# Two convolution blocks made in halves among the last attention heads, with a different opening, in an encoder layer on one core

## The chip, the core and the metric

The kernel runs on one core of a Trainium2 chip, as one program and one launch. Its engines are TensorE (matrix products; PE in the profile, with PEld for the loading of weights), VectorE (DVE), ScalarE (ACT), GpSimd (POOL) and SyncE (SP), which here only issues DMA transfers. Each engine works through its own list of instructions in order, and they wait for each other by semaphores. A transfer waits in the queue of the engine that issues it until its buffer is free, and whatever is behind it in that queue waits too. The metric is device time in microseconds.

## What is computed

One layer of a streaming encoder, in f32, over a sequence of 1024 positions and 1024 features:

```python
mod = (c_act @ w_ada[l] + b_ada[l])[:, None, :]
sh_m, sc_m, g_m, sh_f, sc_f, g_f = jnp.split(mod, 6, axis=-1)
h = rmsnorm(x, norm_mix_w[l]) * (1 + sc_m) + sh_m
z, xbc, dt_raw, q, k, v = jnp.split(h @ w_in[l], IN_SPLITS, axis=-1)
y_ssd = ssd_mixer(z, xbc, dt_raw, ...)
y_att = chunk_attention(q, k, v, rel_bias[l])
x = x + g_m * (jnp.concatenate([y_ssd, y_att], axis=-1) @ w_out[l])
h = rmsnorm(x, norm_ffn_w[l]) * (1 + sc_f) + sh_f
x = x + g_f * conv_ffn(h, w_up[l], ffn_conv_w[l], w_down[l])
return rmsnorm(x, final_norm_w)
```

Two parts matter here. The attention has 8 heads of 64, and a chunk of 64 positions sees itself and the 8 chunks before it, with a relative bias. The SSD mixer begins with a causal convolution over 4 positions and a silu:

```python
xbc = jax.nn.silu(causal_dwconv(xbc, conv_w) + conv_b.astype(xbc.dtype))
```

Its 1024 channels are eight blocks of 128: 0 to 3 are the values, 4 and 5 the two groups of B, 6 and 7 those of C.

## The kernel before

**Products.** A product of two f32 matrices is made as three faster ones: both operands are split into a rounded high part and the rest, and high by high, high by low and low by high are summed in PSUM (`mm3`, lines 79 to 81; the splitting is `split`, lines 88 and 89). A weight tile of 128 output columns over the whole contraction (8 blocks `kt` of 128) is loaded, split and paired in `wu_pair`. The product of such a tile with the 1024 positions is 2 halves of 24 products of 512 columns (`gemm_ft`).

**Order.** The order of instructions on each engine is made by the framework when the kernel is built: a planner simulates the program's times and takes what is ready, the earlier line of the program first. Two things bind it. `tc.issue_after(i)` puts an instruction behind `i` on the same engine, and the wrappers V, A and T (VectorE, ScalarE, TensorE) keep the program's order while their `on` is set.

**Opening.** The modulation is made column by column: `mod_col` loads 128 rows of `w_ada` (512 KB) and one VectorE instruction with an accumulator multiplies them by the activated condition and sums. The rows of x come in eight tiles of 128 (`x_load`, 512 KB each), each is squared (`x_square`), turned into 1/rms (`x_rstd`: an addition of EPS on VectorE, a power on POOL) and scaled (`x_scale`). For each contraction block `kt` the loop at line 409 makes two modulation columns (scale SC_M and shift SH_M), loads a block of the first weights (`w_first`, 384 KB), splits it into `wsh` and `wsl`, turns the block of x on TensorE and applies scale and shift (`h_block`: high part on ScalarE, the f32 value on ScalarE, low part on VectorE). With it go q and k of pairs 0 and 1 (`first_qk`) and v of both (`first_v`). The positions are done in two halves `hh`; the first is made while weights arrive, with the last two blocks after the others. Block 0 of the first half is made in two parts of two row tiles: only x tiles 0 and 1 are loaded ahead of the modulation, tiles 2 and 3 after it. TensorE makes 8 and 12 products of the identity (`warm_up`) before that.

**Attention.** The heads are four pairs. For pair p and each of four steps u, `attn_scores` makes scores for two tiles of 128 positions (`scores`), adds the bias (with the row minimum, line 529), takes the exponential (532), its reciprocal sum (534) and scales on POOL (535). `attn_pv` then turns the probabilities on TensorE (561, 564), splits them and multiplies by v (572, 573); line 578 adds the halves into `ya`. The two bias tiles of a pair are loaded on SP's queue at its beginning and their corners masked by POOL (591, 592). For tiles 0 to 2 of pair 0 a part of the bias is loaded early (`bias_early`). q, k and v of pair 2 are written inside pair 1, those of pair 3 inside pair 2 (`GP`: q and k in step 0, v in step 2), and the planner uses them to fill TensorE. A k or q tile needs parts moved between partitions, by transfers on SP's queue (line 230). Pairs 1 and 2 make one modulation column in each step (through the single buffer `rowb`, after the last reciprocal sum). Pair 3 has no products besides its own; its first two steps load and split the weights of convolution blocks 4 and 6.

**Convolution blocks.** After pair 3, `conv_silu` makes a block: two halves of products into one PSUM tile of two banks, ScalarE's first tap over 1024 positions, three VectorE steps for the other taps (line 636), and silu. The order is 4, 6, 5, 7, then 0 to 3, which are turned back to rows. After each, `conv_mods` makes 2 to 4 modulation columns (CMODS, 24 in all) through three buffers `wos`.

**Memory.** q and k tiles come from one pool of 12 (`qkp`, 4 KB a partition each), used first by x; B, C and the values have pools that are made when the attention's have been closed.

## Time and profile before

| | us |
|---|---|
| median of 3 runs | 1205.41 |
| lowest and highest | 1205.05, 1207.55 |
| profiled execution | 1205.95 |
| its span, first to last instruction | 1204.2 |

The stages on the span: opening and first projections 0 to 98, pair 0 from 98, pairs 1 and 2 to some 235, pair 3 and the convolution blocks to 362, then the z projection, the SSD scan with the output projection from 420, and the feed-forward part from about 540 to the end.

A row of a timeline has the start, the time, the engine, the line, the operation, output and inputs with shapes and count, and in brackets how long the engine had stood idle before and for whom. L61 is the line of the wrappers V, A and T. TensorE's ends are modelled: successive products overlap, so the rate shows in their starts. A busy time counts a product for its whole length. "PEclk" is the granted share of TensorE's clock.

### The profile page before, as it was taken

The page shows a single profiled execution, that of the slowest core. Times are in us where ns is not written, and L with a number is a line of the kernel's source. Part 1 is how long each engine was busy: PE and PEld are TensorE (multiplying, and loading weights), DVE is VectorE, ACT ScalarE, POOL GpSimd, SP SyncE. Part 2 cuts the span into 40 slices and gives each one's busy share as a digit, 9 for nine tenths or more (in the row PEclk, how much of TensorE's full clock was granted, in tenths as well). Part 3 has the DMA queues.
Part 4 walks back from the last instruction along what each step waited for, and adds up shares of the span by engine and source line. Part 5 has one row for each costly group of instructions (what it writes and reads, how often), then busy time and mean ns, then how long its engine had stood idle before and what let it go on. Part 6 is the DMA issues. An engine that isn't in the chain of part 4 may idle for free.

```text
span 1204.2 us, 15722 instructions
## 1 busy us (share of the span) xinstructions
PE 1168.7 (97%) x5823; PEld 980.8 (81%) x5823; DVE 909.1 (75%) x1364; ACT 587.5 (49%) x968; POOL 156.5 (13%) x177
## 2 busy tenths in 40 slices
PE   8998999899999899999999999999999999999996
PEld 6777888788889888888788888888888888888885
DVE  7645565775596888658999988898889879766986
ACT  6534564674243757577534443344333445433454
POOL 1002342530000344200000000000000000000522
PEclk8998999999999989999999999999999999999998
DMA  9635434301486322140232323322233378733443
GB/s 357 244 84 136 110 108 116 108 1 36 153 273 222 124 66 93 53 164 30 79 139 98 102 92 105 131 81 98 94 121 114 110 250 299 258 114 122 158 132 149
DMA packets 61293, 160.24 MB, mean 133 GB/s; under 512 B 6608, under 2 KB 7072, under 8 KB 59808
## 3 DMA queue, kind: packets, MB, share of 16 engines
q1 hardware_dynamic: 54160, 134.85, 34.2%
q10 hardware_dynamic: 7056, 24.38, 5.1%
q8 instruction: 46, 0.75, 0.3%
q14 instruction: 31, 0.25, 0.1%
HBM read 121.15 MB, written 28.61 MB: 124 GB/s over the span
## 4 chain that ended last, share of the span: by engine, by line
PE 85%; DVE 8%; issue 3%; DMA 2%; ACT 1%; SPq 1%; POOL 0%; POOLq 0%; DVEq 0%; ACTq 0%
PE wops L827 6%; PE dn L81 5%; PE dn L79 5%; PE dn L80 5%; PE uY L79 5%; PE uY L81 5%; PE uY L80 5%; PE uX L81 3%; PE uX L79 3%; PE uZ L80 3%; PE uZ L79 3%; PE uX L80 3%; PE uZ L81 3%; PE s L79 3%; PE s L80 3%
## 5 line engine op out<-in xcount | busy, mean ns | idle before, releaser
L80 PE MATMUL dn<-w 128*128 128x512 f32 x296 | 108.1, 392 | 0.0
L79 PE MATMUL dn<-w 128*128 128x512 f32 x296 | 108.1, 391 | 0.0
L81 PE MATMUL dn<-w 128*128 128x512 f32 x296 | 100.2, 391 | 0.2 <-DVE w L89 0.2
L79 PE MATMUL uY<-tH,w 128*128 128x512 f32 x248 | 97.2, 392 | 0.0
L80 PE MATMUL uY<-tL,w 128*128 128x512 f32 x248 | 97.0, 391 | 0.0
L81 PE MATMUL uY<-tH,w 128*128 128x512 f32 x248 | 96.9, 391 | 0.0
L1549 POOL TENSOR_TENSOR ya<-ya,xs 128x512 f32<-128x512 f32 x4 | 17.2, 4330 | 557.6 <-ACT xs L1545 557.6
L88 ACT ACTIVATE w<-ya 128x1024 fp32r<-128x1024 f32 (+1 forms) x41 | 39.2, 957 | 87.3 <-PE uY L81 84.2
L827 PE MATMUL wops<-hH,yhl 128*128 128x512 f32 x224 | 73.4, 401 | 0.0
L81 PEld LDWEIGHTS dn<-w 128*128 128x128 f32 x296 | 55.4, 188 | 13.2 <-DVE w L89 1.1
L79 PEld LDWEIGHTS dn<-w 128*128 128x128 f32 x296 | 55.5, 188 | 12.3
L80 PEld LDWEIGHTS dn<-w 128*128 128x128 f32 x296 | 55.5, 188 | 12.2
L535 POOL TENSOR_SCALAR p<-p,st 128x640 f32<-128x640 f32 (+4 forms) x64 | 49.3, 776 | 108.3 <-DVE st L534 95.2
L529 DVE CUSTOM_DVE_ANT_0 p<-s,bias 128x640 f32<-128x640 f32 (+4 forms) x58 | 38.3, 676 | 29.2 <-PE tp L561 10.3
L88 ACT ACTIVATE w<-xs 128x1024 fp32r<-128x1024 f32 (+1 forms) x41 | 39.1, 954 | 37.3 <-PE uY L81 33.3
L89 DVE TENSOR_TENSOR pt<-tp,pt 128x512 fp32r<-128x512 f32 (+2 forms) x72 | 42.0, 596 | 18.1 <-ACT pt L88 17.7
L81 PEld LDWEIGHTS uY<-tH,w 128*128 128x128 f32 x248 | 46.6, 188 | 10.5
L79 PEld LDWEIGHTS uY<-tH,w 128*128 128x128 f32 x248 | 46.5, 188 | 10.3
L80 PEld LDWEIGHTS uY<-tL,w 128*128 128x128 f32 x248 | 46.6, 188 | 10.2
L79 PE MATMUL s<-hH,wh 128*128 128x512 f32 x128 | 50.6, 395 | 1.2 <-DVE ct L636 1.0
L88 ACT ACTIVATE pt<-tp 128x512 fp32r<-128x512 f32 (+2 forms) x72 | 36.8, 525 | 29.9 <-PE tp L561 15.4
L1223 DVE SCALAR_TENSOR_TENSOR a<-cv,pkt,a 128x1023 f32<-128x1023 f32 (+1 forms) x40 | 51.0, 1277 | 0.1
(492 smaller groups left out, 3422.4 us busy)
## 6 DMA issues: line engine op xcount, KB each, us to landing
wos<-in_w_ada_dram SPq DMA_DIRECT2D x24, 512.0 KB, 4.6
gz<-a ACTq DMA_DIRECT2D x10, 1024.0 KB, 5.0
ya<-in_w_up_dram SPq DMA_DIRECT2D x11, 768.0 KB, 4.1
xs<-in_w_up_dram SPq DMA_DIRECT2D x11, 768.0 KB, 4.3
adat<-in_w_ada_dram SPq DMA_DIRECT2D x16, 512.0 KB, 7.6
raws<-in_w_ft_dram SPq DMA_DIRECT2D x14, 512.0 KB, 3.8
qk<-qk SPq DMA_DIRECT2D x56, 128.0 KB, 2.3
gy<-a ACTq DMA_DIRECT2D x10, 512.0 KB, 2.6
```

The source lines that it names most:

```text
L79: T.matmul(ps, lh, rh, start=start, stop=False, skip_group_check=more)
L80: T.matmul(ps, lh, rl, start=False, stop=False, skip_group_check=more)
L81: T.matmul(ps, ll, rh, start=False, stop=stop, skip_group_check=more)
L88: i = A.activation(hi, src, AF.Copy) if ehi is A else ehi.tensor_copy(hi, src)
L89: return i, elo.tensor_tensor(lo, src, f32(hi), ALU.subtract)
L529: V.tensor_tensor_reduce(out=dst, in0=src, in1=bsl, scale=-1.0, scalar=3e38, op0=ALU.add, op1=ALU.min, accum_out=nm)
L535: G.tensor_scalar(pv_, pv_, rr, 1.0, op0=ALU.mult, op1=ALU.mult)
L827: i = op(*a, **k)
L1223: V.scalar_tensor_tensor(a[:, j:S], c[:, 0:S - j], w[2 - j], a[:, j:S], op0=ALU.mult, op1=ALU.add)
L1549: G.tensor_tensor(src, src, fnr[:, halves[1]], ALU.mult)
```

## The change

It moves work and reorders it; the products of the layer stay the same.

- **Memory**: the 12 tiles come from three pools of 4: one tile of four (`qkx`, x tiles 4 to 7, then k of pairs 1 and 3, later `xs`), four (`qkb`, q and high k of pairs 0 and 2, later B and C), four (`qkt`, x tiles 0 to 3, then the rest).
- **Convolution**: blocks 4 and 6 are made in halves by `conv_half`, one in each step of pair 3, through the one accumulator `acc`. The last three columns of the first half are kept (`edge`) for the second half's taps. Their weights are prepared in the last step of pair 2 and the second of pair 3. Their silu comes after blocks 5 and 7.
- **Modulation columns**: pairs 1 and 2 make 16 instead of 8 (2 in each step; 3, 3, 2, 0), the convolution stage 16 instead of 24.
- **Pair 0**: its bias tiles are issued on ScalarE's queue; all masks are pinned behind normalizations on POOL. In the q product of pair 2, contraction blocks 1, 3 and 5 are pinned behind scores 1, 2 and 3 of pair 0.
- **Opening**: four x tiles ahead of the modulation, block 0 made whole, tiles squared on ScalarE, VectorE, ScalarE, VectorE; EPS is added on ScalarE, or inside VectorE's reduction; 26 products of the identity instead of 12; the modulation columns and the low part of the weights of each block are pinned behind a shift, and block 0's high part goes to VectorE.

```diff
-CMODS = (2, 3, 3, 3, 3, 3, 4, 3)
+AMODS = {1: (2, 2, 2, 2), 2: (3, 3, 2, 0)}
+CMODS = (3, 3, 3, 3, 2, 2)
+GPIN = {1: (0, 1), 3: (0, 2), 5: (0, 3)}
-WARM = (8, 12)
+WARM = (8, 26)
...
     def new_pair(p):
-        qk[p] = {n: [qk_tile(F32R) for _ in range(2)] for n in ("q", "kh", "kl")}
+        if p % 2:
+            k4 = qk_four(F32R)
+            t = [qk_tile(qkt, n) for n in (2, 3)] + [k4[:, n, :] for n in range(4)]
+        else:
+            t = [qk_tile(qkb, n) for n in range(4)] + [qk_tile(qkt, n) for n in (0, 1)]
+        qk[p] = {n: t[2 * i:2 * i + 2] for i, n in enumerate(("q", "kh", "kl"))}
...
         if eng is A:
-            i = norm_to(xts[st], junk, ms)
+            norm_to(xts[st], junk, ms)
+            A.activation(ms, ms, AF.Identity, bias=mhalf[:, 7:8])
...
-    for st in range(2):
+    for st in range(4):
         x_load(st)
...
-    r0 = x_rstd(ms0)
-    r1 = x_rstd(x_square(1, V))
-    x_scale(0, r0, A)
-    x_scale(1, r1, A)
+    x_scale(0, x_rstd(ms0), A)
+    x_scale(1, x_rstd(x_square(1, V)), V)
+    x_scale(2, x_rstd(x_square(2, A)), A)
+    x_scale(3, x_rstd(x_square(3, V)), A)
...
-                mod_col(SC_M + kt, wu.tile([P, 1024], F32, tag="wh", name="adat"))
-                mod_col(SH_M + kt, adw[:, kt % 2, :])
+                at = last_lo.ins if kt == 1 else bm.ins if kt else None
+                mod_col(SC_M + kt, wu.tile([P, 1024], F32, tag="wh", name="adat"), at)
+                mod_col(SH_M + kt, adw[:, kt % 2, :], at)
...
-                split(wsh[:, kt, :], ws_lo(kt), t, A, V)
-                if kt == 0:
-                    for st in (2, 3):
-                        x_load(st)
-                    for b in range(2):
...
+                with tc.issue_after(bm.ins) if not kt else ExitStack():
+                    (A.activation(wsh[:, kt, :], t, AF.Copy) if kt else V.tensor_copy(wsh[:, kt, :], t))
+                with tc.issue_after(bm.ins):
+                    V.tensor_tensor(ws_lo(kt), t, f32(wsh[:, kt, :]), ALU.subtract)
...
-            nc.sync.dma_start(t, bias[2 * p + h])
-            G.memset(t[0:64, 576:640], -1e30)
-            G.memset(t[64:128, 0:64], -1e30)
+            (nc.sync if p else nc.scalar).dma_start(t, bias[2 * p + h])
             bt.append(t)
+
+        def masks():
+            for h, t in enumerate(bt):
+                with tc.issue_after(last_g[-1 if h or not p else -5]):
+                    G.memset(t[0:64, 576:640], -1e30)
+                    G.memset(t[64:128, 0:64], -1e30)
+
+        if p:
+            masks()
         for u in range(4):
             pa = attn_scores(p, 2 * u, bt)
             pb = attn_scores(p, 2 * u + 1, bt)
+            if p + u == 0:
+                masks()
             for fn in extra.get(u, ()):
                 fn()
             if p in (1, 2):
-                mod_col(todo.pop(0), rowb, last_v[0])
-            if p == 3:
-                if u < 2:
-                    early[4 + 2 * u] = wu_pair(w_ft[4 + 2 * u], A, G)
+                for _ in range(AMODS[p][u]):
+                    mod_col(todo.pop(0), rowb, last_v[0])
+            if (p, u) in ((2, 3), (3, 1)):
+                early[2 * p] = wu_pair(w_ft[2 * p], A, G)
...
-    def gemm_ft(wh, wl, outs):
-        for hh in range(2):
+    def gemm_ft(wh, wl, outs, pins={}, hhs=(0, 1)):
+        for hh in hhs:
             for kt in range(KT):
                 w = slice(kt * P, (kt + 1) * P)
-                mm3(c4(outs[hh]), wh[:, w], wl[:, w], *ht(hh, kt), kt == 0, kt == KT - 1)
+                with tc.issue_after(slast[pins[kt]]) if not hh and kt in pins else ExitStack():
+                    mm3(c4(outs[hh]), wh[:, w], wl[:, w], *ht(hh, kt), kt == 0, kt == KT - 1)
...
+    def conv_half(ft, hh):
+        wh, wl = early[ft]
+        ps = psv.tile([P, 512], F32, tag="acc", bufs=1, name="acc")
+        gemm_ft(wh, wl, [ps, ps], hhs=(hh,))
+        w = [pkt[:, SCW + 4 * ft + j:SCW + 4 * ft + j + 1] for j in range(4)]
+        dst = bct[ft][:, 512 * hh:512 * hh + 512]
+        A.activation(dst, ps, AF.Identity, scale=w[3], bias=pkt[:, SCB + ft:SCB + ft + 1])
+        for j in range(1, 4):
+            V.scalar_tensor_tensor(dst[:, j:512], ps[:, 0:512 - j], w[3 - j], dst[:, j:512],
+                                   op0=ALU.mult, op1=ALU.add)
+        if hh == 0:
+            edge[ft] = stat(3)
+            V.tensor_copy(edge[ft], ps[:, 509:512])
+            return
+        for j in range(1, 4):
+            V.scalar_tensor_tensor(dst[:, 0:j], edge[ft][:, 3 - j:3], w[3 - j], dst[:, 0:j],
+                                   op0=ALU.mult, op1=ALU.add)
...
-    mtq += [qk_tile(F32) for _ in range(6)][2:]
-    attention(3)
+    for ft in (4, 6):
+        bc_tile(ft)
+    attention(3, {u: [lambda u=u: conv_half(4 + 2 * (u // 2), u % 2)] for u in range(4)})
...
-    for g in range(2):
-        conv_mods(2 * g, conv_silu(4 + g, bt_[g]))
-        conv_mods(2 * g + 1, conv_silu(6 + g, ct_[g]))
+    for n, ft in enumerate((5, 7)):
+        bc_tile(ft)
+        conv_mods(n, conv_silu(ft, bct[ft]))
+        silu(bct[ft - 1])
```

## What I predicted before the run

> **What bounds the kernel now.** I read the page first, then busy time by stretch, then the timeline of the stretches in which TensorE stands.
>
> ```profile
> span 1204.2 us, 15722 instructions
> PE 1168.7 (97%) x5823; PEld 980.8 (81%) x5823; DVE 909.1 (75%) x1364; ACT 587.5 (49%) x968; POOL 156.5 (13%) x177
> PE 85%; DVE 8%; issue 3%; DMA 2%; ACT 1%; SPq 1%; POOL 0%; POOLq 0%; DVEq 0%; ACTq 0%
> ```
>
> TensorE is the bound: busy 97% of the span, and 85% of the chain that ended last. Nearly all of its products stay as they are in this change, so time can only come from where TensorE stands or is granted half its clock. The next table gives each stretch's length, then busy time (instructions) of PE, PEld, DVE, ACT and POOL, the granted clock, the share of the DMA engines and GB/s.
>
> ```profile
> 10.00:25.00 15.00, 10.93 (x58) 9.54 (x57) 12.67 (x29) 10.26 (x16) 2.74 (x5) 0.77 1.03 407
> 25.00:45.00 20.00, 19.57 (x118) 17.16 (x117) 17.64 (x40) 11.09 (x18) 0.55 (x1) 1.00 0.99 373
> 98.60:105.00 6.40, 6.40 (x34) 5.39 (x33) 2.23 (x12) 2.02 (x8) 0.73 (x2) 1.00 0.83 180
> 105.00:125.00 20.00, 15.92 (x87) 13.78 (x86) 14.75 (x48) 14.21 (x36) 9.10 (x18) 0.83 0.33 92
> 125.00:235.00 110.00, 108.50 (x645) 94.90 (x643) 63.92 (x172) 59.14 (x135) 42.14 (x46) 1.00 0.40 114
> 230.00:265.00 35.00, 30.50 (x196) 25.86 (x196) 28.17 (x84) 27.01 (x67) 15.04 (x20) 0.95 0.07 25
> 265.00:317.00 52.00, 52.00 (x282) 44.76 (x281) 25.03 (x35) 20.83 (x35) 3.15 (x6) 1.00 0.11 31
> 317.00:345.00 28.00, 26.86 (x124) 22.03 (x124) 24.25 (x35) 8.81 (x11) 0.00 (x0) 1.00 0.84 284
> ```
>
> I call lost what a stretch has beyond busy time times granted clock: 15.0 - 10.93 x 0.77 = 6.6 us in the opening (10 to 25), 20.0 - 15.92 x 0.83 = 6.8 us as the first pair of heads begins (105 to 125), 1.5 us in the 110 us after it, 35.0 - 30.50 x 0.95 = 6.0 us in the last pair (230 to 265), nothing while convolution blocks fill TensorE (265 to 317), 1.1 us after that. The change touches just these places, so about 22 us is its ceiling.
>
> **The opening.** Two more row tiles of x are loaded ahead of the first modulation and weight tiles, and block 0 is made whole instead of in two halves. 14 more warm-up products are added, the additions of EPS leave VectorE, and pins keep each block's reductions behind the last shift.
>
> ```profile
> qk<-in_x_dram SPq DMA_DIRECT2D x8, 512.0 KB, 7.0
> 2.59 0.21 ACT L61 ACTIVATE na<-pkt 128x8 f32<-128x8 f32 x1 [0.53 <-DVE pkt L61]
> 7.74 2.84 PE L61 MATMUL warm<-ident 128*128 128x128 f32 x24
> 12.85 0.74 PE L79 MATMUL acc<-hH,wsh 128*128 128x256 f32 x4 [0.86 <-ACT hH L61]
> 24.70 1.10 PE L79 MATMUL acc<-hH,wsh 128*128 128x512 f32 x4
> 46.56 0.15 DVE L204 TENSOR_TENSOR bmix<-modc,pkt 128x1 f32<-128x1 f32 x1
> 48.41 0.78 ACT L289 ACTIVATE hH<-tp,bmix,amix 128x512 fp32r<-128x512 f32 x1 [1.70 <-PE tp L282]
> 50.64 0.39 PE L61 MATMUL vps<-wsh,hL 128*128 128x256 f32 x1 [0.40 <-DVE hL L293]
> ```
>
> Twelve warm-up products are the 24 instructions of 2.84 us; 26 take 2.84 x 26/12 = 6.2 us and run from 7.74 to 13.9. The two x tiles moved forward are 2 x 512 KB, or 2.6 us at 407 GB/s, so block 0 starts about 2.6 us later than at 12.85, at 15.4. But its second half goes with the first: block 0 is 12 products of 512 columns, 0.23 us apart (rows under the last pair), and 12 of 256 at half of that, 4.2 us, so block 1 starts near 20 instead of at 24.70. TensorE is then over 4 us ahead. Most of that isn't kept: the transfers run at 0.99 of their engines until 45, whatever the order, and the last block's shift (bmix) stands at 46.56. What is kept is the wait behind it: ScalarE sat 1.70 us for transposes that were late on TensorE, and these come early now. I take 1.6 us. Bounds: -2.2 us (a slow stretch like 110 to 115 below, 4.43 busy at half clock) and +3.3 us (1.6, and 25 to 45 at 407 GB/s instead of 373: 20 x 0.084 = 1.7). The warm-up fills time in which TensorE has nothing until 15.4. The six additions of EPS that go to ScalarE, busy 10.26 of 15, are as small as its 0.21 us at 2.59: nothing. Block 0's high part moves from ScalarE to VectorE, which holds up only what follows it in block 0.
>
> **The first pair.** Its bias tiles are issued from ScalarE's queue, their masks come after the first two row tiles' normalizations on POOL, and in pair 2's q the products of contraction blocks 1, 3 and 5 must come after scores 1, 2 and 3.
>
> ```profile
> 95.67 7.64 SPq L230 DMA_DIRECT2D qk<-qk  x11
> 105.22 4.58 DMA bias<-in_bias_dram
> 98.50 0.28 PE L61 MATMUL vps<-wsh,hL 128*128 128x256 f32 x1
> 99.24 0.08 DVE L529 DVE_READ_ACCUMULATOR2_ANT st<- 128x1 f32 x1
> 103.39 0.63 PE L271 MATMUL s<-qk 128*128 128x256 f32 x4
> 107.13 0.14 POOL L591 MEMSET bias<- 64x64 f32 x1 [6.02 <-DMA bias<-in_bias_dram]
> 108.10 0.44 PE L564 MATMUL tp<-ident,p 128*128 128x128 f32 x2 [2.46 <-POOL p L535]
> 110.57 0.69 PE L564 MATMUL tp<-ident,p 128*128 128x128 f32 x2 [1.09 <-POOL p L535]
> ```
>
> The bias loads queue behind eleven moves (95.67 to 103.3); POOL meets the masks first and waits 6.02 us, and the probabilities behind them make TensorE wait 2.46 and 1.09 us. Scores 1, whose PSUM is free at 99.3, stand behind 24 products of q until 103.39. In the changed order they start at about 99.4, 4.0 us sooner, with the products left to fill the waits behind them. I take 4 us. Bounds: 0 (the products that filled 98.6 to 103.4 are only spent elsewhere) and the whole 6.8. The issue on ScalarE costs something only if it comes before its buffer is free, after the last v product at 98.50: then the evacuation of v and the exponentials stand behind it. Its transfer took 4.58 us and would land near 103.4, about when row tile 3 first needs it.
>
> A half clock follows an idle stretch:
>
> ```profile
> 105.00:110.00 5.00, 2.03 (x10) 1.16 (x8) 2.28 (x10) 2.24 (x7) 1.06 (x5) 0.93 0.85 274
> 110.00:115.00 5.00, 4.43 (x19) 4.39 (x20) 2.94 (x9) 3.10 (x8) 2.55 (x6) 0.50 0.10 41
> ```
>
> [...]
>
> **The middle.** The reductions for the modulation (a load of a row tile, then one VectorE instruction) go from one in each step of two pairs (8) to 16 in seven steps, through one buffer: 9 of the 16 must wait for the reduction before them and then for a load.
>
> ```profile
> rows<-in_w_ada_dram SPq DMA_DIRECT2D x7, 512.0 KB, 4.5
> L138 DVE CUSTOM_DVE_ANT_0 wos<-wos,rows 128x1024 f32<-128x1024 f32 x17 | 20.5, 1218 | 3.1 <-DMA wos<-in_w_ada_dram 3.1
> ```
>
> Eight more are 8 x 1.3 = 10.4 us with the accumulator read, in a stretch where VectorE idles 110 - 63.9 = 46.1 us. A reduction that meets unlanded data holds up the softmax and evacuations behind it, and the load waits on SP's queue ahead of the q and k moves. I charge -1 us; bounds -4 us (9 waits at 0.45 us) and 0. The unbounded case is a rival.
>
> **The last pair.** Four halves of convolution products come in, with their evacuation; the last reduction leaves.
>
> ```profile
> 224.19 0.40 PE L79 MATMUL acc<-hH,wh 128*128 128x512 f32 x1
> 224.43 0.39 PE L80 MATMUL acc<-hL,wh 128*128 128x512 f32 x1
> 123.13 0.68 DVE L236 SCALAR_TENSOR_TENSOR ev<-acc,qk 128x512 fp32r<-128x512 f32 x1
> 123.86 0.50 PE L79 MATMUL acc<-hH,wh 128*128 128x512 f32 x1 [0.16 <-DVE ev L236]
> 236.03 2.53 POOL L535 TENSOR_SCALAR p<-p,st 128x640 f32<-128x640 f32 x2
> 236.24 1.66 DVE L138 CUSTOM_DVE_ANT_0 rows<-rows 128x1024 f32<-128x1024 f32 x1
> 238.50 0.35 PE L572 MATMUL pv<-pt,v 128*128 128x256 f32 x1 [2.49 <-DVE ya L578]
> ```
>
> A product starts 0.23 us after the one before, so a half of 24 is 5.5 us and four are 22 us, moved here out of the full stretch 265 to 317. They are more than the 6.0 us lost here, 2.49 of which is one wait behind the reduction at 236.24 that is gone. The evacuation of a half is three half-width steps at 0.69 and a copy, about 2.3 us: 9 us on VectorE, which is busy 28.2 of a stretch that grows from 35 to some 50. All halves use one accumulator, so each waits for the evacuation of the last; today's q and k parts do so too and waited 0.16 us at 123.86. I take 5.5 us of the 6.0. Bounds: -2.4 us (three full evacuations of 2.8 us with ScalarE's part, nothing between them: 6.0 - 8.4) and +8 (busy includes short transposes that stand apart, so the loss is larger than my formula says; the two extra microseconds are a guess at it).
>
> **The convolution stretch.** Six whole blocks remain and 16 of 24 reductions. VectorE, 24.25 of 28 us busy from 317, loses 10.4 us of reductions and two blocks' steps; the 1.1 us lost there goes. I take 1 us, bounds -1 and 1.1. The pools keep the same 12 tiles in three groups; the grouped k tiles of a pair end with the same last scores, so nothing.
>
> The sum: 1.6 + 4 - 1 + 5.5 + 1 = 11.1 us. The profiled execution took 1205.95 us around its span of 1204.2, and the median of the runs is 1205.41: 1205.4 - 11.1 = 1194.3.
>
> **Rivals.** First, slower: the waits for the one row buffer decide. Each of 9 reductions holds VectorE for a landing of 4.5 us, and TensorE loses the part in which VectorE had work, 63.9/110 = 0.58: 2.6 us each, 23.5 in all, 22.5 beyond what I charged: 1217. From 1.3 us a wait (12.1/9) the gain is gone. For it: in-order engines and a load that can't start early. Against: DMA is 0.40 busy there and an order that places the reduction late enough pays nothing. Second, the halves do not fill: the attention chain and the single accumulator keep them apart, and the last pair gains nothing: 1194.3 + 5.5 = 1199.8. For it: the order on each engine comes from a planner, not from the text of the program. Against it: the 0.16 us. Third, the pins only move the fill: opening and first pair give nothing, 1194.3 + 5.6 = 1199.9; for it speaks the full DMA until 45, against it the waits on POOL. Second and third together leave 1205.4, no change: the change then doesn't do what it says. Fourth, all terms at the upper bound: 3.3 + 6.8 + 8 + 1.1 = 19.2, or 1186.
>
> **Chances and range.** Forecast 0.48, fourth 0.10, second 0.12, third 0.10, no change 0.06, first 0.14. Faster is 0.48 + 0.10 + 0.12 + 0.10 = 0.80, within 0.2% (2.4 us, about what a measurement of this kernel tells from no change) 0.06, slower 0.14. The low end is 1185, just under the fourth case. The lower bounds add to -2.2 + 0 - 4 - 2.4 - 1 = -9.6, but not all together; 1207 leaves out most of the first rival. The likeliest case alone is 1189 to 1199.
>
> **What would show it.** Opening: block 1 near 20 and the last v products of the first half near 49 instead of 50.64. First pair: scores 1 near 99.4, no mask wait on POOL, clock 1.00 from 105 to 125. Middle: VectorE idle behind loads into rows under 4 us in all. Last pair: convolution products between scores, no wait over 1 us. Wrong if the stretch from 125 to the last pair loses more than 5 us, or if a wait of TensorE on the accumulator exceeds 2 us.

## The result, and the profile after

The changed kernel took 1223.51 us (median of six runs, 1217.48 to 1226.95), the kernel before 1205.74 in the same series (1204.59 to 1207.55): a ratio of 1.014, interval 1.0113 to 1.0166. It is slower by about 17.8 us where 11.1 us of gain were forecast. The profiled execution of the changed kernel is the slowest of its six, 1226.95 us around a span of 1225.2; what follows explains the 21.0 us between the two spans.

Of the page of the changed kernel, the lines that answer to the first three of the prediction:

```profile
span 1225.2 us, 15749 instructions
PE 1177.9 (96%) x5839; PEld 988.6 (81%) x5839; DVE 911.6 (74%) x1371; ACT 598.0 (49%) x978; POOL 157.3 (13%) x178
PE 79%; DVE 10%; DMA 4%; issue 3%; ACT 3%; POOL 1%; SPq 0%; POOLq 0%; DVEq 0%; ACTq 0%
```

TensorE's share of the chain that ended last falls from 85% to 79%; VectorE, DMA and ScalarE gain two each. To find the place, I cut both kernels at the same points of the work: first scores of pair 1, of pair 2, of pair 3, last scores of pair 3, start of the z projection, start of the state-space stage. (In the changed kernel the fifth cut, 351.0, is the last attention step, 3.6 us ahead of the z projection; TensorE is busy all of these 3.6 us, so no loss changes its stage.) (First of the five rows in the fences below: pair 1 as current pair; second: pair 2; third: last pair; fourth: convolution blocks while attention ends; fifth: convolution with the reductions, to the first state-space product.) Busy time by stretch, kernel before, columns as in the prediction:

```profile
122.50:178.90 56.40, 55.50 (x321) 48.21 (x321) 31.97 (x89) 31.15 (x73) 23.10 (x28) 1.00 0.43 116
178.90:232.80 53.90, 52.89 (x319) 46.30 (x317) 32.07 (x84) 28.25 (x65) 19.40 (x19) 1.00 0.38 110
232.80:264.00 31.20, 26.78 (x173) 22.77 (x173) 25.50 (x78) 23.28 (x59) 11.80 (x19) 0.95 0.08 28
264.00:343.00 79.00, 77.95 (x395) 66.00 (x396) 48.24 (x71) 28.64 (x46) 4.04 (x8) 1.00 0.35 114
343.00:421.70 78.70, 73.86 (x528) 68.61 (x527) 59.82 (x100) 41.80 (x87) 11.31 (x8) 0.99 0.59 195
```

The changed kernel, with the stretch from 45 to 55 and its first pair ahead of the same five stages:

```profile
45.00:55.00 10.00, 8.26 (x45) 7.12 (x44) 6.82 (x13) 8.15 (x16) 2.73 (x3) 0.83 0.44 160
...
99.10:105.00 5.90, 5.90 (x32) 4.99 (x31) 3.69 (x20) 3.77 (x13) 1.92 (x6) 1.00 0.86 208
105.00:110.00 5.00, 5.00 (x34) 4.57 (x33) 3.46 (x11) 3.10 (x8) 2.77 (x6) 1.00 0.61 197
110.00:117.10 7.10, 6.91 (x49) 5.92 (x47) 7.04 (x23) 7.00 (x18) 3.02 (x4) 1.00 0.01 3
...
117.10:180.90 63.80, 59.80 (x341) 51.80 (x341) 37.02 (x100) 32.73 (x74) 22.42 (x29) 0.97 0.43 124
180.90:253.10 72.20, 62.85 (x335) 54.20 (x334) 41.57 (x102) 31.46 (x70) 22.27 (x24) 0.91 0.46 133
253.10:299.60 46.50, 42.42 (x241) 36.29 (x240) 29.68 (x84) 33.57 (x66) 9.22 (x16) 0.93 0.04 12
299.60:351.00 51.40, 51.40 (x277) 44.16 (x277) 25.11 (x41) 21.22 (x37) 3.18 (x7) 1.00 0.12 37
351.00:441.40 90.40, 80.01 (x547) 73.30 (x545) 66.80 (x108) 43.60 (x89) 11.38 (x8) 0.96 0.59 196
```

With the prediction's measure (length less busy time times granted clock) the five stages of the kernel before lost 0.9, 1.0, 5.8, 1.1 and 5.6 us; those of the changed kernel lose 5.8, 15.0, 7.0, 0.0 and 13.6. The first pair, from 99.1, loses 0.2 us where it lost 6.8, and the last v product ahead of it starts at 99.08 instead of 98.50. The account is then: +0.6 before the first pair, -6.6 in it, +18.9 in pairs 1 and 2, +1.2 in the last pair, +6.9 in the two convolution stages, 21.0 together. That it meets the 21.0 exactly is chance, for the clock has two digits. By lengths alone the changed kernel is 5.4 us ahead where pair 1 begins (117.10 against 122.50), 25.1 slower over the five stages (324.3 against 299.2) and 1.3 slower behind them. The first pair kept its promise; pairs 1 and 2 took it back three times over.

What TensorE missed there shows in the timeline of the changed kernel (start, length, engine, line; idle time before and its releaser in brackets; SPq is SP's sequencer, and its length is the time it stood at those issues):

```profile
181.47 5.44 SPq L242 DMA_DIRECT2D qk<-ev  x2
182.03 1.21 DVE L141 CUSTOM_DVE_ANT_0 rows<-rows 128x1024 f32<-128x1024 f32 x1
183.72 0.69 DVE L91 TENSOR_TENSOR pt<-tp,pt 128x512 fp32r<-128x512 f32 x1
187.00 0.54 SPq L139 DMA_DIRECT2D rows<-in_w_ada_dram  x1
190.77 1.39 DVE L141 CUSTOM_DVE_ANT_0 rows<-rows 128x1024 f32<-128x1024 f32 x1 [6.36 <-DMA rows<-in_w_ada_dram]
192.44 1.22 PE L283 MATMUL s<-qk 128*128 128x256 f32 x4 [3.25 <-DVE st L535]
```

This is one round of the loop. The reduction at 182.03 frees the row buffer at about 183.2. Its next load can't be issued: SP stands at two moves of q from 181.47 to 186.9, and the load is behind them in the same queue. It goes out at 187.00 and lands 3.8 us later. VectorE, which works in order, has done its last step at 184.4 (183.72 and 0.69), meets the next reduction and stands idle for 6.36 us, with the softmax of the next row tile behind it; and TensorE waits 3.25 us until that softmax has read the scores and their PSUM is free.

This round isn't the rule in one respect. Of the 15 loads behind a reduction, it is the only one that left more than 0.9 us after its buffer was free; most left at once. The other waits are nearly all landing, 3.7 us in the median, in front of a reduction that comes sooner than that. TensorE's longest wait is such a one:

```profile
216.65 1.98 DVE L141 CUSTOM_DVE_ANT_0 rows<-rows 128x1024 f32<-128x1024 f32 x1 [3.36 <-DMA rows<-in_w_ada_dram]
219.29 0.58 PE L579 MATMUL pv<-pt,v 128*128 128x256 f32 x1 [3.99 <-DVE pt L91]
```

This load left at 212.89, right behind the reduction that freed its buffer (211.63, 1.23 long). VectorE stands for 3.36 us, with the splitting of the probabilities behind it, and TensorE for 3.99. The two rounds, each in a stretch of 10 us:

```profile
188.00:198.00 10.00, 6.75 (x30) 5.93 (x29) 4.76 (x14) 3.42 (x9) 3.06 (x3) 0.67 0.49 135
214.00:224.00 10.00, 6.01 (x24) 5.13 (x23) 6.15 (x12) 3.73 (x9) 2.52 (x2) 0.73 0.56 157
```

They lose 5.5 and 5.6 us, more than half of the 20.8 of pairs 1 and 2; only the first has to do with the queue. The table of waits of the changed kernel, from 118 to 255, for VectorE and for SP from 118 to 253 (total, times, longest):

```profile
DVE rows L141 <- DMA rows<-in_w_ada_dram: 23.3, 10, 6.4
SPq L139 <- DVE modc L141: 23.5, 5, 5.2
```

VectorE waits for rows ten times. The kernel before has no such wait in the list of its pairs 1 and 2. It goes both ways: SP waits 23.5 us for reductions to free the buffer, and moves that q and k need stand behind it. But no wait of TensorE or VectorE for these moves is in the list, and the spaced kernel below has nearly the same wait of SP without the loss.

### The profile page after: what moved, and what is told of

The parts are those of the page before. It is cut to its first block, busy times and chain, and to the rows that moved or that the text cites. A ratio compares the mean times of both kernels' runs of the same rounds, so it can differ in the third digit from the quotient of the medians.

```text
span 1225.2 us, 15749 instructions
## 1 busy us (share of the span) xinstructions
PE 1177.9 (96%) x5839; PEld 988.6 (81%) x5839; DVE 911.6 (74%) x1371; ACT 598.0 (49%) x978; POOL 157.3 (13%) x178
## 4 chain that ended last, share of the span: by engine, by line
PE 79%; DVE 10%; DMA 4%; issue 3%; ACT 3%; POOL 1%; SPq 0%; POOLq 0%; DVEq 0%; ACTq 0%
PE wops L868 6%; PE dn L83 5%; PE dn L81 5%; PE dn L82 5%; PE uY L81 4%; PE uY L83 4%; PE uY L82 4%; PE uX L83 3%; PE uZ L82 3%; PE uX L81 3%; PE uX L82 3%; PE uZ L81 3%; PE uZ L83 3%; PE acc L81 2%; PE acc L82 2%
## 5 line engine op out<-in xcount | busy, mean ns | idle before, releaser
L1590 POOL TENSOR_TENSOR ya<-ya,qkx 128x512 f32<-128x512 f32 x4 | 17.2, 4334 | 557.7 <-ACT qkx L1586 557.7
L541 POOL TENSOR_SCALAR p<-p,st 128x640 f32<-128x640 f32 (+4 forms) x64 | 46.6, 733 | 167.4 <-DVE st L540 146.2
L90 ACT ACTIVATE w<-qkx 128x1024 fp32r<-128x1024 f32 (+1 forms) x41 | 39.1, 954 | 37.3 <-PE uY L83 33.3
L90 ACT ACTIVATE pt<-tp 128x512 fp32r<-128x512 f32 (+2 forms) x72 | 36.4, 524 | 42.8 <-PE tp L567 21.7
L81 PE MATMUL acc<-hH,wh 128*128 128x512 f32 x128 | 54.4, 425 | 1.4 <-DVE qk L257 0.8
L538 ACT ACTIVATE p<-p,st 128x640 f32<-128x640 f32 (+4 forms) x64 | 44.1, 690 | 18.2 <-DVE st L535 17.5
L82 PE MATMUL acc<-hL,wh 128*128 128x512 f32 x128 | 52.9, 413 | 0.0
```

Source lines behind the costliest of these rows:

```text
L81: T.matmul(ps, lh, rh, start=start, stop=False, skip_group_check=more)
L82: T.matmul(ps, lh, rl, start=False, stop=False, skip_group_check=more)
L90: i = A.activation(hi, src, AF.Copy) if ehi is A else ehi.tensor_copy(hi, src)
L538: A.activation(pv_, pv_, AF.Exp, scale=-1.0, bias=nm, accum_out=rs)
L541: last_g.append(G.tensor_scalar(pv_, pv_, rr, 1.0, op0=ALU.mult, op1=ALU.mult).ins)
L1590: G.tensor_tensor(src, src, fnr[:, halves[1]], ALU.mult)
```

## The experiments

Each kernel was timed beside the kernel before on the same chip, whose median there was 1205.89 to 1206.94 us; ratios and intervals are to that. Where a time is set against "the changed kernel", its 1223.51 is meant.

**Columns back to one in a step.** The changed kernel, with the old number of columns in pairs 1 and 2:

```diff
-AMODS = {1: (2, 2, 2, 2), 2: (3, 3, 2, 0)}
-CMODS = (3, 3, 3, 3, 2, 2)
+AMODS = {1: (1, 1, 1, 1), 2: (1, 1, 1, 1)}
+CMODS = (4, 4, 4, 4, 4, 4)
```

> The changed kernel with one modulation column in each step of pairs 1 and 2 (8) and 4 after each of six convolution blocks (24). Theory L (reductions hold VectorE while their load is under way): VectorE waits under 4 us for loads into rows between 99 and 255 instead of 21 us, pair 3's first scores come near 235 instead of 253, and the kernel gains 10 to 18 us on the changed one; 24 reductions after the late end of attention may cost up to 8 x 1.2 = 10 us of that. Rival V (VectorE's time itself, 8 x 1.3 us): gains 10 us at most and nothing after the convolution stage. Rival H (the convolution halves delay the attention chain): no gain, within 3 us of the changed kernel.

Measured: 1205.29, ratio 0.9987 (0.9975 to 0.9998). 18 us come back. But with the gain of the first pair still in it, it should lie below the kernel before by more than 1.7 us: something else in the change costs. It stands in the last stage, which loses 86.80 - 76.37 x 0.95 = 14.2 us here, with 24 columns in six blocks, instead of 5.6; pair 2 loses 0.9.

**Reductions without their loads.** The changed kernel, in which the 16 reductions of pairs 1 and 2 stay but read the activated condition in place of a loaded row; the loads are left out, so these 16 modulation columns aren't computed.

```diff
-                    mod_col(todo.pop(0), rowb, last_v[0])
+                    ft = todo.pop(0)
+                    with tc.issue_after(last_v[0]):
+                        V.tensor_tensor_reduce(out=rowb, in0=rowa, in1=rowa, ...
+                                               accum_out=modc[:, ft:ft + 1])
```

> The changed kernel with the 16 reductions of pairs 1 and 2 kept but their loads of w_ada rows left out (the activated condition stands in for the rows, so modulation columns of the gates and the feed-forward scale are other numbers). Theory L: 15 to 20 us faster than the changed kernel, near 1205, pair 3's first scores near 234. Rival V: the same time as the changed kernel within 3 us, since VectorE does the same instructions. A third way (the loads hold the moves on SP's queue rather than VectorE): also faster, but then the trace of the changed kernel should show scores waiting for moves, which it does not.

Measured: 1211.31, ratio 1.0039 (1.0026 to 1.0052), 12 us below the changed kernel, less than the 15 to 20 that I had expected. The stages tell more than the total: pairs 1 and 2 lose 1.9 and 1.0 us, as good as all of the 18.9 is back, while VectorE still does 16 reductions there. So the work isn't the price, the loads are. The two stages behind the last pair, however, lost 20.3 us in this run. The longest wait of TensorE there has nothing to do with reductions:

```profile
PE zps L81 <- ACT wzh L90: 5.9, 1, 5.9
```

ScalarE's splitting of a z weight block waited 5.5 us for its load, and TensorE for that; the ten us around it (340 to 350) lose 7.5. Why the load came late there, and the rest of the 20.3, stay open.

**The columns alone.** The kernel before with 16 columns in pairs 1 and 2 (same places as in the change) and two in each of its eight blocks:

```diff
-CMODS = (2, 3, 3, 3, 3, 3, 4, 3)
+AMODS = {1: (2, 2, 2, 2), 2: (3, 3, 2, 0)}
+CMODS = (2, 2, 2, 2, 2, 2, 2, 2)
...
-                mod_col(todo.pop(0), rowb, last_v[0])
+                for _ in range(AMODS[p][u]):
+                    mod_col(todo.pop(0), rowb, last_v[0])
```

> The kernel of before with the changed kernel's columns alone: 16 in pairs 1 and 2 (2 a step, then 3, 3, 2, 0) and 2 after each of eight convolution blocks. Theory L: 12 to 20 us slower than before, with over 10 us of VectorE idle behind loads into rows. Rival V: up to 3 us slower, or faster by 1 us for the convolution stage. Rival O (only the opening or the halves make the loads late): within 3 us of before.

Measured: 1223.01, ratio 1.0134 (1.0115 to 1.0152): 16.1 of the 17.8 us, without anything else of the change. Its pairs 1 and 2 lose 63.90 - 60.44 x 0.97 = 5.3 and 67.40 - 56.83 x 0.90 = 16.3 us, much as in the changed kernel (5.8 and 15.0). VectorE's wait for rows in this run, 118 to 255:

```profile
DVE rows L139 <- DMA rows<-in_w_ada_dram: 21.4, 9, 5.3
```

Nine waits, as the prediction had counted them, and 2.4 us each.

**The first pair alone.** The kernel before with the bias issue on ScalarE's queue, the masks behind the normalizations, and the pins in pair 2's q:

```diff
-            nc.sync.dma_start(t, bias[2 * p + h])
-            G.memset(t[0:64, 576:640], -1e30)
-            G.memset(t[64:128, 0:64], -1e30)
+            (nc.sync if p else nc.scalar).dma_start(t, bias[2 * p + h])
...
+            if p + u == 0:
+                masks()
...
+        gemm_ft(wh, wl, outs, GPIN if (p, which) == (2, 0) else {})
```

> The kernel of before with the pair 0 part alone: bias tiles issued on ScalarE's queue, masks behind normalizations, products of contraction blocks 1, 3 and 5 behind scores 1, 2, 3. My prediction charged it 4 us of gain (0 to 6.8): near 1201.5, scores 1 near 99.4, no half clock between 105 and 125. Rival F (filler only moved): within 1.5 us of before, with the wait standing later.

Measured: 1200.97, ratio 0.995 (0.9932 to 0.9968): 6.0 us faster.

**The opening alone.** The kernel before with the opening's part of the change:

```diff
-WARM = (8, 12)
+WARM = (8, 26)
...
-    for st in range(2):
+    for st in range(4):
         x_load(st)
...
-                    for b in range(2):
...
-                        hb = h_block(0, 0, (2 * b, 2 * b + 1))
...
+                at = last_lo.ins if kt == 1 else bm.ins if kt else None
```

> The kernel before with the opening of the change alone (four x tiles first, block 0 whole, 26 warm-up products, EPS off VectorE, the pins). Prediction's step: 1.6 us faster, 1205.3 beside the 1206.9 that the kernel before took with the first four experiments, last v product about 1.6 us before 98.50. Rival (transfers full until 45, so the order buys nothing, and two row tiles ahead of the weights delay block 0): within 1 us of before, 1206 to 1208, block 0's first product near 17 instead of 12.85, last v product 98 to 99.

Measured: 1202.40 (1198.87 to 1207.77, twelve runs), ratio 0.997 (0.9957 to 0.9982). It is faster, so my rival, that nothing comes of it, falls; block 0 does begin later, at 16.72, and the gain is larger than the 1.6 us of the prediction. The profiled execution is the slowest of the twelve; the last section returns to that.

**The halves alone.** The kernel before with the pools and the four halves: the changed kernel without its opening and first pair, and with AMODS and CMODS of the first experiment.

> The kernel before with the three pools and the four convolution halves in the last pair alone: 8 modulation columns in pairs 1 and 2 as before, 24 in the six remaining blocks, no change in opening or first pair. Prediction's steps: last pair 5.5 and convolution stretch 1 faster, 1200.4. Rival (the halves run as closed runs of 24 products while the attention chain waits, the chain's end moves back some 20 us and with it the memory of the buffers from which the convolution stretch's columns are reduced, which then pile up on VectorE): 3 to 5 us slower, 1210 to 1212, with 7 to 9 us still lost between the first scores of pair 3 and its last transposes.

Measured: 1211.01, ratio 1.0039 (1.0024 to 1.0053): 4.2 us slower. Last pair and last stage of this run, by stretch, and the wait of TensorE that is new in the latter:

```profile
232.80:283.10 50.30, 45.83 (x264) 39.45 (x263) 33.49 (x91) 36.02 (x71) 10.69 (x16) 0.93 0.04 12
...
337.50:426.80 89.30, 76.23 (x532) 70.88 (x530) 70.81 (x118) 40.65 (x83) 12.21 (x9) 0.94 0.68 223
```

```profile
PE zps L81 <- DVE wzl L87: 6.1, 1, 6.1
```

The last pair loses 50.30 - 45.83 x 0.93 = 7.7 us where it lost 5.8: TensorE's busy time grew by 19 us of convolution products, and the time it loses didn't shrink. The last stage loses 17.6 instead of 5.6. VectorE is busy 70.81 us of it instead of 59.82, because 24 columns now belong to six blocks. The 6.1 us are a wait for a z weight block's low part (393.95). In VectorE's line it stands behind the last reductions (to 386.3) and behind the scaling of output weights, for whose factors VectorE had stood 3.91 us.

**The same 16 columns, spaced.** The changed kernel with two columns in every step, one pinned behind each row tile:

```diff
-AMODS = {1: (2, 2, 2, 2), 2: (3, 3, 2, 0)}
+AMODS = {1: (2, 2, 2, 2), 2: (2, 2, 2, 2)}
...
             pa = attn_scores(p, 2 * u, bt)
+            if p in (1, 2):
+                mod_col(todo.pop(0), rowb, last_v[0])
             pb = attn_scores(p, 2 * u + 1, bt)
...
-                for _ in range(AMODS[p][u]):
+                for _ in range(AMODS[p][u] - 1):
```

> The changed kernel with its 16 columns of pairs 1 and 2 dealt out evenly: two in every step, one behind each of the step's two row tiles instead of both behind the second; the number of columns, loads and reductions is the same. If the waits for loads through the one row buffer cost the 18 us, a load now has half a step, some 6 us against a landing of 4.5 to 5.5, and most waits go: 1207 to 1214, waits of VectorE for rows under 10 us in all. If it is the 8 more reductions as VectorE's work that costs, or any reduction between two row tiles holds the softmax, nothing comes back: 1220 or more.

Measured: 1202.41, ratio 0.9963 (0.9951 to 0.9976): 21 us below the changed kernel and faster than the kernel before, more than I had expected. Its five stages by stretch, and its wait for rows from 118 to 255:

```profile
115.60:173.60 58.00, 55.19 (x321) 47.90 (x321) 36.16 (x97) 31.56 (x72) 24.40 (x29) 1.00 0.49 140
173.60:232.00 58.40, 57.58 (x335) 49.52 (x333) 37.88 (x98) 30.74 (x70) 23.79 (x23) 1.00 0.52 152
232.00:284.70 52.70, 46.71 (x265) 39.96 (x264) 34.36 (x93) 35.72 (x71) 10.08 (x17) 0.94 0.06 20
284.70:339.00 54.30, 54.30 (x286) 46.40 (x286) 29.94 (x44) 22.17 (x37) 2.40 (x5) 1.00 0.21 70
339.00:420.20 81.20, 74.74 (x531) 69.17 (x529) 61.31 (x102) 41.61 (x87) 11.31 (x8) 1.00 0.58 195
```

```profile
DVE rows L141 <- DMA rows<-in_w_ada_dram: 7.8, 7, 2.4
```

Losses: 2.8, 0.8, 8.8, 0.0 and 6.5 us. VectorE's busy time in pairs 1 and 2 is close to that of the changed kernel (36.16 and 37.88 against 37.02 and 41.57), and the number of reductions and loads is the same; the distance between two of them differs, and with it the order around them. SP stands for reductions nearly as long (from 115 to 232) as in the changed kernel (23.5 us), so this standing isn't what costs:

```profile
SPq L139 <- DVE modc L141: 21.7, 5, 6.4
```

The last stage, with the same 16 columns and the same code as in the change, nearly has its old loss again (6.5 against 13.6; 5.6 before).

**One column less beside the first pair's part.** The kernel of 1200.97 with the last column of pair 2 in the first convolution block instead:

```diff
-CMODS = (2, 3, 3, 3, 3, 3, 4, 3)
+CMODS = (3, 3, 3, 3, 3, 3, 4, 3)
...
-            if p in (1, 2):
+            if p == 1 or p == 2 and u < 3:
```

> The kernel before with the first pair's part of the change (1201.0 alone) and with one modulation column less in pair 2: the last one, whose reduction stood at 236.24 before a 2.49 us wait of TensorE, goes to the first convolution block. If that wait is worth its length, 1198.5 to 1199.5; if another step of the attention chain waits in its place, 1200.5 to 1201.5.

Measured: 1201.49, ratio 0.996 (0.9944 to 0.9976): no gain. The last pair loses 4.5 us where the kernel of 1200.97 loses 5.9, and the convolution stretch behind it 5.7 instead of 2.4. The first half of the expectation falls; by these losses the wait was moved.

**Opening and first pair.** Both parts on the kernel before, with nothing of the rest (the edits of the two experiments together):

> The kernel before with the opening and the first pair of the change together, and nothing of the rest: 8 columns in pairs 1 and 2, eight whole convolution blocks, one pool. If the two parts add (ratios 0.997 and 0.995 alone), 0.992 of before, near 1197. If both only reorder the same lost time ahead of the second pair, the better of the two alone, 0.995, near 1201.

Measured: 1198.91 (1198.34 to 1201.37), ratio 0.9946 (0.9934 to 0.9959): the lowest median of all, and better than both kernels. It lies between the two expectations. Over the first pair alone the opening adds 2.1 us by the medians and 0.5 by the ratios (0.9946 against 0.995), and the intervals overlap: that it adds anything there is not shown.

**The same with 16 spaced columns.** Two columns in each step as in the spaced kernel, `CMODS = (2, 2, 2, 2, 2, 2, 2, 2)`:

> The run before this one in the list (opening and first pair) with 16 columns in pairs 1 and 2 instead of 8, two in each step, one behind each row tile, and two instead of three in each of eight whole convolution blocks. If spaced columns cost little, within 3 us of that run, 1196 to 1200, and against the changed kernel with spaced columns (1202.4) it shows what the four halves cost: 2 to 6 us. If the columns cost even when spaced and the halves gave that back, 1202 or more.

Measured: 1202.28, ratio 0.9971 (0.9958 to 0.9984): at the edge of the second expectation. Eight more columns cost 3.4 us by the medians even when spaced, though the intervals just meet (up to 0.9959, from 0.9958). The profiles show only a part: pairs 1 and 2 lose 2.4 us instead of 1.8, and the last stage, with fewer columns, 5.5 instead of 5.9. The spaced kernel (1202.41, interval 0.9951 to 0.9976) differs from this one by the halves: with 16 spaced columns no cost or gain of theirs is seen.

**Halves in two parts.** The spaced kernel with contraction blocks 0 to 3 of each half given out behind the step's first row tile:

```diff
+            if p == 3:
+                conv_quarter(4 + 2 * (u // 2), u % 2)
             pb = attn_scores(p, 2 * u + 1, bt)
...
+    def conv_quarter(ft, hh):
+        ps = quarter[ft, hh] = psv.tile([P, 512], F32, tag="acc", bufs=1, name="acc")
+        gemm_ft(*early[ft], [ps, ps], hhs=(hh,), kts=range(4))
```

> The changed kernel with spaced columns (1202.4), and each convolution half given out in two parts: the products of contraction blocks 0 to 3 behind the step's first row tile, 4 to 7 and the evacuation behind its second. If the halves don't fill the last pair because each runs as one closed block of 24 products, eight smaller blocks hide 2 to 5 us more: 1197.5 to 1200.5. If the chain of softmax, transposes and attention products sets the pace whatever stands beside it, 1201.5 to 1203.5.

Measured: 1201.03 (1199.76 to 1201.20), ratio 0.9954 (0.9942 to 0.9967), between the two expectations. Its last pair:

```profile
229.80:280.30 50.50, 45.23 (x265) 38.44 (x264) 33.84 (x93) 35.75 (x70) 11.15 (x17) 0.97 0.07 21
```

6.6 us lost, 2.2 fewer than in the spaced kernel and still more than the 5.8 before. Over the whole kernel the difference from the spaced one (1202.41) is within the intervals. Neither expectation is settled by this; that the chain of softmax, transposes and attention products sets the pace is the likelier of the two, since most of the loss stays.

**Another queue for the loads.** The changed kernel, columns in pairs and threes as they were, their loads issued by ScalarE:

```diff
-                    mod_col(todo.pop(0), rowb, last_v[0])
+                    mod_col(todo.pop(0), rowb, last_v[0], nc.scalar)
```

> The changed kernel with the loads of its 16 columns in pairs 1 and 2 issued by ScalarE instead of SP; number, buffer and place of the reductions as in the change. In the changed kernel the load behind the 6.36 us wait stood 3.8 us in SP's queue behind two moves (reduction done at 183.16, load issued at 187.00) and needed 3.7 us to land. If the queue is what makes the waits long, about half of the 21 us between the changed kernel and the spaced one comes back: 1210 to 1216, waits of VectorE for rows near 12 us instead of 23. If the landing behind the one buffer alone decides, waits stay near 20 us and the time at 1218 to 1226; the same if ScalarE, held by the wait for the buffer, delays the exponentials instead.

Measured: 1206.84, ratio 1.0012 (0.9997 to 1.0026): 16.7 us below the changed kernel, more than I had expected of the queue. Pairs 1 and 2 by stretch, and the wait for rows from 118 to 250:

```profile
115.30:176.80 61.50, 58.37 (x341) 50.59 (x341) 37.00 (x100) 32.91 (x74) 23.36 (x29) 1.00 0.46 131
176.80:236.20 59.40, 55.48 (x318) 47.49 (x317) 38.65 (x99) 29.38 (x68) 23.37 (x23) 1.00 0.52 158
```

```profile
DVE rows L141 <- DMA rows<-in_w_ada_dram: 17.9, 9, 4.1
```

The waits are nearly as many, 17.9 us against 23.3, the longest 4.1 instead of 6.4; the stages lose 3.1 and 3.9 us instead of 5.8 and 15.0. The waits are nearer to what the second theory had, the time is not. So it isn't the sum of the waits that TensorE pays, nor the length of one. TensorE's longest wait in these two pairs stands behind VectorE's longest, 4.1 us:

```profile
207.11 0.36 PE L578 MATMUL pv<-pt,v 128*128 128x256 f32 x1 [1.85 <-DVE ya L584]
```

Here 4.1 us of a standing VectorE cost TensorE 1.85; in the changed kernel 3.36 us cost it 3.99. By these two rounds it matters which step stands behind the wait and how many products are ready beside it. Behind the long waits the clock falls as well (0.50 from 193 to 198 and from 219 to 224 in the changed kernel; over the two stages 0.97 and 0.91 there, 1.00 here); that share is 59.80 x 0.03 + 62.85 x 0.09 = 7.5 of the changed kernel's 20.8 us. Of the 16.7 us, the queue's delay of 3.8 us before one load directly explains at most the 5.5 of its round. Why the rest went is not shown: the round of the 3.99 had no such delay.

## Why the prediction was wrong

**What bounds the kernel, and the account by stages,** held: TensorE is the bound, and the losses by stage add up to the difference of the spans within their rounding.

**The first pair, 4 us, bounds 0 and 6.8:** right, and near its upper bound: 6.0 us alone. In the changed kernel:

```profile
99.89 0.65 PE L283 MATMUL s<-qk 128*128 128x256 f32 x4
105.27 0.14 POOL L606 MEMSET bias<- 64x64 f32 x1 [0.91 <-DMA bias<-in_bias_dram]
```

Scores 1 start at 99.89 where I had said 99.4, the mask waits 0.91 us instead of 6.02 and has normalizations ahead of it, and the clock is 1.00 from 99.1 to 117.1. Of the 6.8 us that I had taken as the upper bound, 0.2 are still lost there: 6.6 came in the profiled execution.

**The opening, 1.6 us, bounds -2.2 and 3.3:** the sign was right where the opening stands alone (3.6 us, 0.3%); on top of the first pair a gain is not shown (0.5 to 2.1 us), and in the profiled execution of the changed kernel it is -0.6. A step in it failed: block 1 starts at 23.57, not near 20.

```profile
17.32 2.07 PE L81 MATMUL acc<-hH,wsh 128*128 128x512 f32 x4 [0.76 <-DVE wsl L63]
23.57 1.09 PE L81 MATMUL acc<-hH,wsh 128*128 128x512 f32 x4
47.98 0.78 ACT L303 ACTIVATE hH<-tp,bmix,amix 128x512 fp32r<-128x512 f32 x1 [0.80 <-DVE bmix L211]
```

Block 0 starts 4.47 us later than before, where I had reckoned 2.6 us for the transfer of two x tiles, and at a low clock: 0.55 granted from 17.0 to 19.5 and 1.00 from 22 to 24 (four products in 2.07 us, 1.09 in block 1). What I took the gain from, ScalarE's 1.70 us for late transposes, did go: it now waits 0.80 us for the last shift (bmix) alone. In this execution that shift itself is late, and hH stands at 47.98 instead of 48.41, 0.4 us of the 1.6. In the kernel with opening and first pair, where block 0 begins at 16.11 and not at 17.32, it stands where I had put it, 1.65 us sooner:

```profile
46.76 0.78 ACT L293 ACTIVATE hH<-tp,bmix,amix 128x512 fp32r<-128x512 f32 x1 [0.87 <-DVE bmix L206]
```

So the step that I named can give the size of the term, and the execution shown of the changed kernel didn't collect it.

**The middle, -1 us, bounds -4 and 0:** this is the step that failed. "9 of the 16 must wait for the reduction before them and then for a load" was counted right. The price failed: "9 waits at 0.45 us" as the lower bound, and -1 us as the term, had no row behind them. The sentence ahead of them set the eight reductions against VectorE's idle 46.1 us, as if a wait could be laid into it. An idle share says how much time an engine has, not when. The wait stands at a given place in an in-order queue, with the softmax of the next row tile behind it. Measured: 18.9 us more lost in pairs 1 and 2, over ten waits 1.9 us each; the same columns alone cost 16.1 us, and spacing them took 21 us off the changed kernel. The first rival had the mechanism right, at a chance of 0.14. That its size was near (2.6 us each, 23.5 us) is partly luck: it let each wait last 4.5 us and charged TensorE 0.58 of it, and the waits lasted 2.3 us in the mean (23.3 over ten), of which TensorE paid 0.81 (18.9 of 23.3). Of the two arguments that I set against it, "DMA is 0.40 busy" asked for the amount that the 16 engines move, and not for how long one load takes to land (3.7 us) behind a buffer that has only just come free. The other, that "an order that places the reduction late enough pays nothing", is nearly what the spaced kernel shows; but the change didn't have that order, with two and three columns behind one another. And of the load that "waits on SP's queue ahead of the q and k moves" I had named one half; the other, the load that stands itself behind moves, occurs once (187.00).

Which engine issues the loads counted for more than the time to start them. Issued by ScalarE instead of SP, the 16 loads took 16.7 us off the changed kernel, though one took as long from issue to landing, 3.7 us in the median in both. Starting a load took 0.33 us of SP's time in the median, some 5 us for 16, so more than that was saved. SP no longer stands for reductions, and a load no longer behind moves; but the spaced kernel keeps 21.7 us of the former and loses only 3.6 us in pairs 1 and 2, and the latter delayed one load of fifteen. Which way the rest came is open; the order of work around the loads differs as well.

**The last pair, 5.5 us of the 6.0:** not delivered; this was the second rival. It lost 5.8 us and loses 7.0 with the halves, 7.7 with the halves alone. The products are there (busy 42.42 us against 26.78), but not where TensorE waits. Its waits there (1.28, 1.46 and 0.72 us, at 255.43, 268.45 and 270.41) are for VectorE's steps of the attention chain; the longest behind an evacuation of a half is 0.18. I had reckoned the filling from amounts again, and from one wait of 0.16 us on the accumulator, which indeed was no hindrance.

**The convolution stretch, 1 us, bounds -1 and 1.1:** wrong by sign: the two stages behind the last pair lost 6.7 us and now 13.6. I had ended my stretch at 345 and counted less work for VectorE. But four halves of convolution products within the attention move its end back, from 317.6 to 351.0 in this kernel, and only then are the columns loaded:

```profile
350.65 1.28 SPq L139 DMA_DIRECT2D wos<-in_w_ada_dram  x3
352.27 1.28 DVE L676 SCALAR_TENSOR_TENSOR xst<-s,pkt,xst 128x1023 f32<-128x1023 f32 x1 [0.82 <-ACT xst L674]
354.39 1.23 DVE L141 CUSTOM_DVE_ANT_0 wos<-wos,rows 128x1024 f32<-128x1024 f32 x1 [0.24 <-DMA wos<-in_w_ada_dram]
356.74 1.21 DVE L141 CUSTOM_DVE_ANT_0 wos<-wos,rows 128x1024 f32<-128x1024 f32 x1
359.02 1.22 DVE L141 CUSTOM_DVE_ANT_0 wos<-wos,rows 128x1024 f32<-128x1024 f32 x1
361.50 0.79 PE L81 MATMUL s<-hH,wh 128*128 128x512 f32 x1 [5.28 <-DVE xst L676]
```

Three columns come between the three steps of one block, the block's one PSUM tile is free 9 us after the start of the first step, and TensorE, whose products last for only 4 of these, waits 5.28 us. In the spaced kernel the loads begin as abruptly (332.06) and three columns stand at the same places, but TensorE has products for 7 of 8 us and waits 0.96. So the late columns cost only where little else is ready beside them, and that the later end of attention alone costs is not shown. Why the run without loads lost 20.3 us in these two stages is settled only for the 7.5 of them named there.

**The sum.** Of the terms, 4 came (6.0 alone, 6.6 in the changed kernel) and 1.6 came alone (3.6) but not in the changed kernel (-0.6); -1 was -18.9, 5.5 was -1.2, and 1 was -6.9. From the fastest kernel to the changed one: 1198.9 with opening and first pair; 1202.3 with 16 spaced columns; 1202.4 with the halves; 1223.5 with the columns put together in pairs and threes.

## What to carry to other kernels

A load into a buffer that the last reader had only just left was a wait of a queue's delay (3.8 us in one round) plus a landing (3.7 us in the median), and everything behind it on VectorE, which works in order, waited too (6.36 us at most): space such steps by at least that time. That took 21 us off here; another queue took 16.7, more than the delay that it removes explains. Price a wait at its place, by what stands behind it and what is ready beside it; the idle share of the engine, or of the transfers, doesn't price it. And when work is moved into an earlier stage, ask what the later end of that stage holds back (here, the loads of the next columns).

## What the runs showed of the hardware that I had not expected

**The same code was granted 0.83 of the clock in one kernel and 1.00 in another.** The stretch from 45 to 55, in which TensorE waits for the last block, in the opening alone and in opening with first pair (the same code there):

```profile
45.00:55.00 10.00, 8.04 (x45) 7.07 (x44) 6.55 (x13) 8.22 (x16) 2.73 (x3) 0.83 0.36 124
```

```profile
45.00:55.00 10.00, 8.29 (x51) 6.95 (x50) 6.82 (x13) 7.99 (x15) 2.74 (x3) 1.00 0.35 120
```

Nearly the same busy time, clock 0.83 and 1.00, and the last v product at 97.98 and 96.16. The changed kernel, whose opening is the same, fell on the slow side (0.83, with 1.00 from 45 to 50, 0.77 to 52.5 and 0.55 to 55; last v product at 99.08). TensorE's waits in this stretch are 1.18, 0.17 and 0.40 us there and 1.14, 0.17 and 0.40 in opening with first pair; so the lower clock came here without a wait over 1.2 us, and nearly the same waits stood at 1.00. Over the twelve runs of the opening alone the mean clock goes from 0.986 (span 1206.1) to 0.993 (span 1197.1): its times spread by 9 us, where those of the kernel before, in 21 runs beside it, spread by 6. That the stretch shown makes this spread is not shown, since one execution of each kernel was profiled.
